# Three of seven reads of the first down products by ScalarE and Pool; the norms' last two squares summed by TensorE

## The chip, the cores and the metric

The kernel runs on one core of a Trainium2 chip, in one launch. The metric is the device time of that core in microseconds (us): 1850.29 us, the median of three executions (1849.76 to 1850.89). One more execution was taken by the profiler and took 1851.48 us; all rows below come from it.

## The reference

One decoder layer over 1024 tokens of width 1024, in fp32, with one sequence:

```
h = modulate(rms_norm(x, norm_ffn1), mod[0], mod[1])
x = x + 0.5 * mod[2] * swiglu(h, gate1, up1, down1)
h = modulate(rms_norm(x, norm_mix), mod[3], mod[4])
x = x + mod[5] * (concat(gated_delta_rule(h), pooled(h)) @ w_out)
h = modulate(rms_norm(x, norm_ffn2), mod[6], mod[7])
x = x + 0.5 * mod[8] * swiglu(h, gate2, up2, down2)
out = rms_norm(x, final_norm)
swiglu(h) = (silu(h @ w_gate) * (h @ w_up)) @ w_down      # hidden width 2816
rms_norm(x, g) = x * rsqrt(mean(x * x) + 1e-6) * g
```

## The kernel before, in words

Activations lie transposed: sixteen tiles A[d, h] of 128 features by 512 tokens, d from 0 to 7 and h the half of the tokens. Every fp32 product is three matmuls on operands that are split into a high and a low fp32r part (tiles named `split` for weights; pairs in H, G, U and zs for what moves). "Stage 1" and "stage 2" are the two SwiGLU blocks; between them stands the mixer.

**Seven products.** The big products of a stage take 2x2 blocks and spend seven block products where eight are usual. `seven` (l. 872) goes through them in the order p1, p2, p5, p6, p3, p7, q4. p1, p6, p7 and q4 of one step share one PSUM bank (tile `mm`) and add onto it, p5 and p3 share another (`po`), and p2 has one of its own (`po`). So p6 may begin only when p1's sum was read, p7 when p6's was, and p3 when p5's was; these are the flags ("read", stage, step, product). Steps 0 to 19 of a stage are the gate and up products, steps from 20 on (`NP1`) are the down products. Step 20 sums over one pair of hidden blocks, 21 over two, 22 over three, then four, so a product of these steps is 3, 6, 9 and 12 matmuls of 512 columns.

**Reading a down product.** `down_read` (l. 979) adds each of the seven sums, times the gate `fg`, onto the tile of A that it belongs to, by one `scalar_tensor_tensor` of VectorE: p1 and p2 onto block (0,0), p6 and p3 onto (0,1), p5 and p7 onto (1,1), q4 onto (1,0). The tiles of A were put away in DRAM and come back by `rest_load` (l. 1186, tiles `A<-xpark` and `A<-rest`), each into a slot that a task of the stage before it has given back.

**The two norms between the stages.** `square_task` (l. 1296) squares the eight feature tiles of one half of the tokens on ScalarE; GpSimd (Pool) adds each onto the first one. `norm_task` (l. 1309) then waits for the last of these additions, lets TensorE take the column sums against a column of ones (four columns of 128 tokens, by `column_sums`, l. 310), VectorE makes mean and epsilon of them (`rx`), Pool raises to the power -1/2, VectorE spreads the result on a diagonal (`row_diag`), and TensorE multiplies it by ones into R, the scale of every token on all partitions (`aux<-cv,ones`). From R and A come the next products' H. This runs for the mixer's norm (1) and the second SwiGLU's norm (2), each for both halves; the final norm has code of its own. TensorE meanwhile has the last products of the stage in its queue.

**The order.** The code is written as generator tasks that yield what they need and what they cost: `("V", 0.77)` asks for 0.77 us of VectorE, S is ScalarE, G Pool, D a DMA on SyncE's queue; `need` takes a buffer, `flag` waits for an event. A class `Order` (l. 36) plays these tasks against each other on the build machine, and the instructions are issued in the order that comes out. This fixes the order on every engine. All calls pass one helper, so that each row of the profile names line L161; what a row belongs to is told by its tiles.

Of the kernel before, what the change touches and what calls it, by code (L numbers as in the profile page):

```python
# [11 lines left out]
ALU = mybir.AluOpType  # L12
AX = mybir.AxisListType

P = 128
D = 1024
T = 1024
HT = 512
KT = D // P
# [3 lines left out]
EPS = 1e-6  # L23
# [12 lines left out]
class Order:  # L36
# [18 lines left out]
    def spawn(self, gen, rank):  # L55
        self.seq += 1
        self.tasks.append({"gen": gen, "rank": rank, "seq": self.seq, "ready": self.t, "ask": None, "last": None, "end": self.t})
        return self.tasks[-1]

    def put(self, what, n=1):  # L60
        self.events.append((self.t, "put", what, n))
# [81 lines left out]
def hybrid_layer_kernel(  # L143
# [22 lines left out]
    V, S, G, PE = Pin(nc.vector, "V"), Pin(nc.scalar, "S"), Pin(nc.gpsimd, "G"), Pin(nc.tensor, "PE")  # L166
    uid = [0]

    def nm(s):
        uid[0] += 1  # L170
        return f"{s}_{uid[0]}"
# [12 lines left out]
    def bank(tag="mm"):  # L184
        bufs = {"mm": 2, "aux": 3, "rec": 1, "po": 2}[tag]
        return psum.tile([P, HT], F32, tag=tag, bufs=bufs, name=nm(tag))

    def pm():
        return work.tile([P, HT], F32, tag="pm", bufs=4, name=nm("pm"))

    def cvt(n=HT):
        return work.tile([P, n], F32, tag="cv", bufs=4, padded_shape=[P, 528], name=nm("cv"))
# [11 lines left out]
    def cst(shape, name):  # L204
        return const.tile(shape, F32, tag=name, name=name)
# [12 lines left out]
    for i, s in enumerate(LEVELS):  # L218
        nb = P // (2 * s)
        v = lmask[:, i].rearrange("p (b two s) -> p b two s", two=2, s=s)[:, :, 0, :]  # L220
# [22 lines left out]
    A = {}  # L243
# [10 lines left out]
    ps = bank("po")  # L254
# [9 lines left out]
    fg = [cst([P, 8], f"fg{i}") for i in range(2)]  # L264
# [30 lines left out]
    def ad():  # L295
        return work.tile([P, HT], F32, tag="ad", bufs=6, name=nm("ad"))
# [7 lines left out]
    def xtile(k, h, src):  # L304

        if k >= KT // 2:
            return gtile(8 + 2 * (k - KT // 2) + h)
        return ztile() if h else ad()

    def column_sums(parts, ps):  # L310
        for n in range(parts[0].shape[1] // P):
            for e, t in enumerate(parts):
                PE.matmul(ps[:, n : n + 1], lhsT=t[:, n * P : (n + 1) * P], rhs=ones[:, 0:1], start=(e == 0), stop=(e == len(parts) - 1))
# [10 lines left out]
    def row_diag(r):  # L324
        diag = cvt()
        V.tensor_tensor(diag.rearrange("p (n j) -> p n j", n=4), ident.unsqueeze(1).broadcast_to([P, 4, P]), r.unsqueeze(2).broadcast_to([P, 4, P]), op=ALU.mult)
        return diag
# [43 lines left out]
    spawn, put, mark = order.spawn, order.put, order.set  # L371

    def need(what, n=1):
        return ("need", what, n)

    def flag(*key):
        return ("flag", key)
# [28 lines left out]
    def release(i):  # L406
        free.append(i)
        put("tmp")
# [358 lines left out]
    rest = (xpark, {})  # L767
# [16 lines left out]
    NP1 = 2 * (NPAIR - 1)  # L784
# [194 lines left out]
    def down_read(st, n, v, ps, banks):  # L979
        d = 2 * plans[st][n]["d"]  # L980
        todo = {"p1": (0, 0), "p2": (0, 0), "p5": (1, 1), "p6": (0, 1), "p3": (0, 1), "p7": (1, 1), "q4": (1, 0)}[v]
        a = d + todo[0], todo[1]
        yield flag("mod", 8 if st else 2)
        yield flag("rest", st, a)
        yield ("V", 0.77)
        V.scalar_tensor_tensor(A[a], ps, fg[st][:, a[0] : a[0] + 1], A[a], op0=ALU.mult, op1=ALU.add)
        if v in ("p2", "p3"):
            put("po")
        elif v == "q4":
            put("mm")  # L990
        else:
            mark(("read", st, n, v))
        if n == len(plans[st]) - 1 or d // 2 not in [e["d"] for e in plans[st][n + 1 :]]:
            mark(("summed", st, a, v))
# [220 lines left out]
    def last_pair():  # L1215
        for h in range(2):
            for d in range(KT):
                yield need("mm")
                ps = bank()
                yield flag("unit", "last", d // 2)  # L1220
                u = unit["last", d // 2]
                for f in range(2):
                    yield flag("G", 0, NS, f, h)
                    for e, (a, b) in enumerate(((0, 0), (0, 1), (1, 0))):
                        yield ("PE", 0.2267)
                        PE.matmul(ps, lhsT=u[:, a, f, (d % 2) * P : (d % 2 + 1) * P], rhs=ring[0, NS, f, h][b], start=f == e == 0, stop=f == 1 and e == 2)
                if h == 1 and d % 2:
                    put("split")
                spawn(last_read(ps, d, h), 0.8)
            spawn(norm_task(h, 1, last_parts[h], A, 1), 1.5)  # L1230

    def last_read(ps, d, h):
        for v in {(0, 0): ("p2",), (0, 1): ("p3",), (1, 0): ("q4",), (1, 1): ("p7",)}[d % 2, h]:
            yield flag("summed", 0, (d, h), v)
        yield ("V", 0.66)
        V.scalar_tensor_tensor(A[d, h], ps, fg[0][:, d : d + 1], A[d, h], op0=ALU.mult, op1=ALU.add)
        put("mm")
        spawn(square_task(1, h, d, last_parts[h], A[d, h]), 2)
        yield ("D", 0.5)
        park[d, h] = dram.tile([P, HT], F32, tag=f"park{d}_{h}", name=nm("park"))  # L1240
        nc.sync.dma_start(out=park[d, h], in_=A[d, h])
# [42 lines left out]
    def low_task(k, h, i, xn):  # L1284
        yield ("S", 0.61)
        ht = htile(k, h)
        H[k, h] = ht
        b = mod[3 * i][:, k : k + 1]
        S.activation(ht[:, 0], xn, AF.Identity, bias=b)
        yield ("V", 0.66)  # L1290
        V.scalar_tensor_tensor(ht[:, 1], xn, b, ht[:, 0].bitcast(F32), op0=ALU.add, op1=ALU.subtract)
        if i == 1:
            put("pm")
        mark(("H", i, k, h))

    def square_task(st, h, i, parts, src):
        yield need("cv" if i else "U")
        yield ("S", 0.52)
        sq = cvt() if i else work.tile([P, HT], F32, tag="U", bufs=4, name=nm("acc"))
        S.activation(sq, src, AF.Square)  # L1300
        parts.append(sq)
        if i:
            yield flag("sum", st, h, i - 1)
            yield ("G", 1.6)
            G.tensor_tensor(parts[0], parts[0], sq, op=ALU.add)
            put("cv")
        mark(("sum", st, h, i))

    def norm_task(h, i, parts, src, rank):
        yield flag("sum", i, h, KT - 1)  # L1310
        yield flag("acol", i)
        yield need("aux", 2)
        yield need("cv")
        yield ("PE", 0.9)
        ps = bank("aux")
        column_sums(parts[:1], ps)
        yield ("V", 0.07)
        r = small.tile([P, 4], F32, tag="rx", bufs=2, name=nm("rx"))
        V.tensor_scalar(r, ps[:, 0:4], 1.0 / D, EPS, op0=ALU.mult, op1=ALU.add)
        put("aux")  # L1320
        put("U")
        yield ("G", 1.0)
        G.tensor_tensor(r, r, neghalf[:, 0:4], op=ALU.pow)
        yield ("V", 0.6)
        diag = row_diag(r)
        yield ("PE", 0.86)
        R = bank("aux")
        PE.matmul(R, lhsT=ones, rhs=diag, start=True, stop=True)
        put("cv")
        for k in range(KT):  # L1330
            if i == 1:
                yield need("pm")
            elif k < KT // 2:
                yield need("zs" if h else "ad")
            elif h == 0:
                yield flag("mix", 3, 1)
            yield ("V", 0.66)
            xn = pm() if i == 1 else xtile(k, h, src)
            XN[k, h] = xn
            V.scalar_tensor_tensor(xn, src[k, h], acol[i][:, k : k + 1], R, op0=ALU.mult, op1=ALU.mult)  # L1340
            if i == 2:
                release(OUT_TILES[h][k])
            spawn(low_task(k, h, i, xn), rank)
        put("aux")
# [446 lines left out]
    def out_task(ps, d, h):  # L1791
        yield flag("mod", 5)
        yield ("V", 0.66)
        V.scalar_tensor_tensor(A[d, h], ps, mod[5][:, d : d + 1], A[d, h], op0=ALU.mult, op1=ALU.add)
        put("mm")
        spawn(square_task(2, h, d, out_parts[h], A[d, h]), 2)
        yield ("D", 0.5)
        rest[1][d, h] = dram.tile([P, HT], F32, tag=f"rest{d}_{h}", name=nm("rest"))
        nc.sync.dma_start(out=rest[1][d, h], in_=A[d, h])
# [206 lines left out]
    for j, piece in enumerate(((0, 0, HT), (1, 0, 256), (1, 256, HT))):  # L2006
        h, lo, hi = piece
        parts, ds = [], list(range(KT))[:: -1 if j % 2 else 1]
        for d in ds:
            if d // 2 not in kept:  # L2010
                kept[d // 2] = wunit2(last_src(ffn2_down, d // 2))
            ps = bank()[:, : hi - lo]
# [3 lines left out]
            a = A[d, h][:, lo:hi]  # L2016
# [32 lines left out]
```

## Time and profile before

| | us | share |
|---|---|---|
| median of three executions | 1850.29 | |
| profiled execution | 1851.48 | |
| its span | 1849.8 | |
| TensorE (PE) busy | 1796.6 | 97% |
| VectorE (DVE) busy | 1400.4 | 76% |
| ScalarE (ACT) busy | 768.4 | 42% |
| GpSimd (POOL) busy | 286.0 | 15% |

Busy time is that of an engine's instructions; what is left of the span is the time in which the engine waited. In a row of the timeline the first two columns are start and duration in us, then engine, line, operation, output and inputs by tile names, shape and count; a bracket at the end gives the idle time ahead of the row and what ended it. PEclk is the granted share of TensorE's full clock. Stage 1's down products run from 483 us on, norm 1 stands at 690 to 735, the mixer's inner part at 735 to 1125, norm 2 at 1125 to 1210, stage 2's down products begin at 1600.

### The profile page before, as it was taken

To read this page: it belongs to the slowest core of one execution; us is meant where nothing else is said; L and a number is where in the kernel's file an instruction comes from. 1 tells how busy PE (TensorE), PEld (TensorE's weight loads), DVE (VectorE), ACT (ScalarE), POOL (GpSimd) and SP (SyncE) were. 2 spreads that over 40 slices of the span, in tenths; PEclk is the share of its full clock that TensorE was granted. 3 is DMA by queue.
4 is the path that set the end of the run, shared out by engine and by line. 5 is a ranking of instruction groups with operands and counts; after the bars stand their busy time and mean duration, and the time that the engine had idled before them with its cause. 6 is when DMAs were issued, how large, how long until landed. Compare 5 with 4: busy or idle time off the path is not lost.

```text
span 1849.8 us, 25078 instructions
## 1 busy us (share of the span) xinstructions
PE 1796.6 (97%) x8511; PEld 1481.7 (80%) x8511; DVE 1400.4 (76%) x2440; ACT 768.4 (42%) x1519; POOL 286.0 (15%) x228
## 2 busy tenths in 40 slices
PE   7999999999999999999999999999999999999997
PEld 6788878888788877788888878878878888778876
DVE  4997888887778878988787666677787666776666
ACT  5454444443422224662443354444445444422225
POOL 2231121201100003120211122212111111100004
PEclk9999999999999999999999999999999999999999
DMA  9534676574679933331111155334455543667722
GB/s 315 182 120 159 207 225 206 182 229 132 201 242 331 310 96 104 103 78 43 31 48 49 41 173 159 95 123 139 154 180 181 174 137 126 206 207 253 238 70 92
DMA packets 307551, 293.29 MB, mean 159 GB/s; under 512 B 28053, under 2 KB 215506, under 8 KB 307424
## 3 DMA queue, kind: packets, MB, share of 16 engines
q1 hardware_dynamic: 306848, 290.57, 49.5%
q8 instruction: 67, 1.10, 0.2%
q0 software_dynamic: 576, 1.13, 0.2%
q14 instruction: 60, 0.49, 0.1%
HBM read 208.53 MB, written 83.10 MB: 158 GB/s over the span
## 4 chain that ended last, share of the span: by engine, by line
PE 83%; DVE 11%; issue 2%; ACT 1%; POOL 1%; DMA 1%; ACTq 0%; POOLq 0%; DVEq 0%
PE mm L161 47%; PE po L161 27%; PE aux L161 7%; PE rec L161 3%; DVE pm L161 2%; DVE A L161 2%; DVE ad L161 2%; DVE split L161 2%; DVE G L161 1%; DVE cv L161 1%; DVE H L161 1%; ACT A L161 0%; DMA G<-in_gdn_norm 0%; DVE zs L161 0%; ACT junk L161 0%
## 5 line engine op out<-in xcount | busy, mean ns | idle before, releaser
L161 PE MATMUL mm<-H,split 128*128 128x512 f32 (+1 forms) x3096 | 766.2, 395 | 9.6 <-DVE H L161 4.0
L161 PEld LDWEIGHTS mm<-H,split 128*128 128x128 f32 x3096 | 568.4, 189 | 127.1 <-DVE H L161 5.1
L161 PE MATMUL po<-H,split 128*128 128x512 f32 x1584 | 388.1, 392 | 4.4 <-DVE H L161 3.0
L161 PEld LDWEIGHTS po<-H,split 128*128 128x128 f32 x1584 | 297.3, 189 | 69.2 <-DVE H L161 4.2
L161 PE MATMUL mm<-G,split 128*128 128x512 f32 x1440 | 342.5, 390 | 4.3 <-ACT split L161 4.3
L161 PEld LDWEIGHTS mm<-G,split 128*128 128x128 f32 x1440 | 269.9, 188 | 61.2 <-ACT split L161 5.2
L161 ACT CAST split<-pm 128x512 fp32r<-128x512 f32 (+3 forms) x264 | 151.7, 582 | 329.0 <-DVE pm L161 322.8
L161 POOL TENSOR_TENSOR A<-A,A 128x512 f32<-128x512 f32 x80 | 130.7, 1644 | 692.2 <-DVE A L161 593.5
L161 DVE TENSOR_TENSOR split<-pm,split 128x512 fp32r<-128x512 f32 (+3 forms) x264 | 176.6, 676 | 45.1 <-ACT split L161 44.5
L161 ACT CAST split<-raw 128x512 fp32r<-128x512 f32 (+2 forms) x199 | 117.6, 596 | 194.0 <-PE mm L161 104.0
L161 PE MATMUL po<-U,split 128*128 128x512 f32 x480 | 155.5, 390 | 2.1 <-DVE A L161 2.1
L161 DVE SCALAR_TENSOR_TENSOR A<-mm,fg,A 128x512 f32<-128x512 f32 (+1 forms) x144 | 103.0, 719 | 65.8 <-PE mm L161 64.5
L161 DVE TENSOR_TENSOR split<-raw,split 128x512 fp32r<-128x512 f32 (+2 forms) x199 | 132.3, 675 | 21.1 <-ACT split L161 20.7
L161 DVE TENSOR_TENSOR A<-A,A 128x512 fp32r<-128x512 f32 (+1 forms) x180 | 124.1, 697 | 4.3 <-ACT A L161 1.2
L161 PEld LDWEIGHTS po<-U,split 128*128 128x128 f32 x480 | 90.1, 188 | 22.0 <-issue 1.7
L161 POOL TENSOR_TENSOR acc<-acc,cv 128x512 f32<-128x512 f32 (+1 forms) x46 | 56.1, 1219 | 292.2 <-ACT cv L161 291.2
L161 ACT CAST split<-cv 128x512 fp32r<-128x512 f32 (+1 forms) x96 | 57.1, 595 | 94.0 <-PE po L161 52.2
L161 DVE TENSOR_TENSOR A<-A,po 128x512 f32<-128x512 f32 x86 | 58.8, 684 | 46.4 <-PE po L161 43.2
L161 PE MATMUL po<-zs,split 128*128 128x512 f32 x240 | 93.4, 389 | 0.0
L161 DVE SCALAR_TENSOR_TENSOR ad<-ad,cs,ad 128x512 f32<-128x512 f32 x98 | 82.8, 845 | 3.5 <-DMA ad<-in_w_ada 2.6
L161 DVE TENSOR_TENSOR split<-cv,split 128x512 fp32r<-128x512 f32 (+1 forms) x96 | 62.7, 653 | 27.7 <-ACT split L161 27.7
L161 ACT CAST A<-A 128x512 fp32r<-128x512 f32 x120 | 72.8, 619 | 25.9 <-DVE A L161 25.2
(279 smaller groups left out, 1881.2 us busy)
## 6 DMA issues: line engine op xcount, KB each, us to landing
gd<-A SPq DMA_DIRECT2D x240, 256.0 KB, 3.9
H<-gd SPq DMA_DIRECT2D x144, 256.0 KB, 3.9
ad<-in_w_ada SPq DMA_DIRECT2D x112, 256.0 KB, 3.3
raw<-in_ffn_gate SPq DMA_DIRECT2D x88, 256.0 KB, 4.0
cv<-in_ffn_up SPq DMA_DIRECT2D x80, 256.0 KB, 4.4
G<-gd SPq DMA_DIRECT2D x64, 256.0 KB, 3.7
raw<-in_w_in SPq DMA_DIRECT2D x40, 256.0 KB, 3.2
cv<-in_ffn_down SPq DMA_DIRECT2D x32, 256.0 KB, 4.0
```

The lines of the kernel that those rows point to most:

```text
L161: ins = f(*args, **kwargs)
```

## The change

Two edits. In `down_read`, p1, p6 and p7 of steps 20, 21 and 22 (nine of the reads of each stage) are no longer one VectorE instruction: ScalarE multiplies the PSUM sum by the gate into a tile of the ring `ad`, sets the read flag, and Pool adds that tile onto A. In `square_task` and `norm_task`, the squares of the last two feature tiles are no longer added by Pool; TensorE takes the column sums of three tiles (the sum so far and the two squares) into twelve columns, and VectorE adds the three by one `tensor_reduce` ahead of the `tensor_scalar` that was there. The planner's price of a Pool addition in `square_task` goes from 1.6 to 1.3.

```
@@ down_read
         a = d + todo[0], todo[1]
         yield flag("mod", 8 if st else 2)
+        if n < NP1 + 3 and v in ("p1", "p6", "p7"):
+            yield need("ad")
+            yield ("S", 0.62)
+            t = ad()
+            S.mul(t, ps, fg[st][:, a[0] : a[0] + 1])
+            mark(("read", st, n, v))
+            yield flag("rest", st, a)
+            yield ("G", 1.4)
+            G.tensor_tensor(A[a], A[a], t, op=ALU.add)
+            put("ad")
+            return
         yield flag("rest", st, a)
         yield ("V", 0.77)
         V.scalar_tensor_tensor(A[a], ps, fg[st][:, a[0] : a[0] + 1], A[a], op0=ALU.mult, op1=ALU.add)
@@ square_task
         parts.append(sq)
-        if i:
+        if 0 < i < KT - 2:
             yield flag("sum", st, h, i - 1)
-            yield ("G", 1.6)
+            yield ("G", 1.3)
             G.tensor_tensor(parts[0], parts[0], sq, op=ALU.add)
             put("cv")
         mark(("sum", st, h, i))
@@ norm_task
     def norm_task(h, i, parts, src, rank):
-        yield flag("sum", i, h, KT - 1)
         yield flag("acol", i)
         yield need("aux", 2)
+        ps = bank("aux")
+        for j, e in enumerate((KT - 3, KT - 2, KT - 1)):
+            yield flag("sum", i, h, e)
+            yield ("PE", 0.9)
+            column_sums((parts[e if j else 0],), ps[:, 4 * j : 4 * j + 4])
+            if j:
+                put("cv")
         yield need("cv")
-        yield ("PE", 0.9)
-        ps = bank("aux")
-        column_sums(parts[:1], ps)
-        yield ("V", 0.07)
+        yield ("V", 0.3)
         r = small.tile([P, 4], F32, tag="rx", bufs=2, name=nm("rx"))
-        V.tensor_scalar(r, ps[:, 0:4], 1.0 / D, EPS, op0=ALU.mult, op1=ALU.add)
+        V.tensor_reduce(r, ps[:, 0:12].rearrange("p (j n) -> p n j", n=4), axis=AX.X, op=ALU.add)
+        V.tensor_scalar(r, r, 1.0 / D, EPS, op0=ALU.mult, op1=ALU.add)
         put("aux")
```

Because the planner plays all tasks again, instructions move on every engine, most of all inside the mixer. Three places follow, two on VectorE and one on TensorE. A tile's number at the end of its name tells one tile from the next; numbers differ between the two kernels.

VectorE in stage 1's down step 22, before: `zs_4612` is the low part of p5's last operand, `po_4744` is p2's sum and `po_4765` is p5's.

```order
619 L161 TENSOR_TENSOR H_0_942_4605<-A_911_4495,H_0_942_4605 128x512
620 L161 TENSOR_TENSOR zs_4612<-A_919_4529,U_4611 128x512
621 L161 SCALAR_TENSOR_TENSOR A_937_4588<-mm_4700,fg_165,A_937_4588 128x512
622 L161 SCALAR_TENSOR_TENSOR A_906_4476<-mm_4582,fg_165,A_906_4476 128x512
623 L161 TENSOR_TENSOR pm_4755<-raw_4499,raw_4570 128x384
624 L161 TENSOR_TENSOR split_4748<-cv_4652,split_4748 128x512
625 L161 SCALAR_TENSOR_TENSOR A_937_4588<-po_4744,fg_165,A_937_4588 128x512
626 L161 TENSOR_TENSOR split_4761<-pm_4755,split_4761 128x384
627 L161 TENSOR_TENSOR split_4770<-raw_4580,split_4770 128x384
628 L161 TENSOR_TENSOR G_949_4627<-A_924_4547,G_948_4626 128x512
629 L161 SCALAR_TENSOR_TENSOR A_979_4743<-po_4765,fg_165,A_979_4743 128x512
630 L161 TENSOR_TENSOR split_4785<-cv_4698,split_4785 128x512
```

The same place after: `zs_4694` is the low part, `po_4738` p2's sum and `po_4765` p5's.

```order
616 L161 SCALAR_TENSOR_TENSOR A_960_4679<-po_4738,fg_165,A_960_4679 128x512
617 L161 TENSOR_TENSOR split_4757<-pm_4740,split_4757 128x384
618 L161 TENSOR_TENSOR split_4762<-cv_4622,split_4762 128x512
619 L161 TENSOR_TENSOR split_4770<-raw_4582,split_4770 128x384
620 L161 TENSOR_TENSOR zs_4694<-A_919_4529,U_4693 128x512
621 L161 TENSOR_TENSOR G_973_4719<-A_931_4575,G_972_4718 128x512
622 L161 TENSOR_TENSOR H_1_980_4742<-A_880_4332,H_1_980_4742 128x512
623 L161 TENSOR_TENSOR G_990_4778<-A_890_4378,G_989_4777 128x512
624 L161 TENSOR_TENSOR H_1_992_4784<-A_955_4656,H_1_992_4784 128x512
625 L161 TENSOR_TENSOR split_4804<-cv_4753,split_4804 128x512
626 L161 TENSOR_TENSOR pm_4824<-cv_4653,cv_4670 128x512
627 L161 SCALAR_TENSOR_TENSOR A_995_4794<-po_4765,fg_165,A_995_4794 128x512
```

The low part stood five rows ahead of the read of p2's sum and now stands four rows behind it; the read of p5's sum came nine rows after the low part and now comes seven rows after it, with six additions from SBUF to SBUF in between.

TensorE at norm 1, first half of the tokens, after: `acc` is the sum of six squares, the two `cv` are the last squares, `aux<-cv,ones` is R, and `mm<-H_1` are stage 1's last products.

```order
1857 L161 MATMUL mm_6453<-H_1_1247_6092,split_6299 128x512
1858 L161 MATMUL aux_6444<-ones,acc_6356 128x1 x4
1859 L161 MATMUL aux_6444<-ones,cv_6442 128x1 x4
1860 L161 MATMUL aux_6444<-ones,cv_6455 128x1 x4
1861 L161 MATMUL mm_6453<-H_1_1247_6092,split_6299 128x512 x2
1862 L161 MATMUL mm_6453<-H_1_1252_6124,split_6299 128x512 x3
1863 L161 MATMUL mm_6483<-H_1_1247_6092,split_6303 128x512 x3
1864 L161 MATMUL mm_6483<-H_1_1252_6124,split_6303 128x512 x3
1865 L161 MATMUL mm_6497<-H_1_1247_6092,split_6303 128x512 x3
1866 L161 MATMUL aux_6504<-cv_6492,ones 128x512
```

Before, twelve such matmuls stood between the column sums and R, and nine behind R; now fourteen stand between them, and the column sums come earlier among the products.

VectorE at the start of stage 2, before: `split_11125` is the first weight split of the product that follows norm 2 (step 0's p1), `zs` and `G` are operands of stage 2's other products.

```order
1676 L161 TENSOR_TENSOR zs_11132<-ad_10606,U_11131 128x512
1677 L161 SCALAR_TENSOR_TENSOR G_2323_11028<-G_2323_11028,mod_159,ad_10593 128x512
1678 L161 TENSOR_TENSOR G_2347_11147<-G_2317_11003,G_2346_11146 128x512
1679 L161 SCALAR_TENSOR_TENSOR G_2325_11035<-G_2325_11035,mod_159,ad_10606 128x512
1680 L161 TENSOR_TENSOR G_2349_11159<-G_2323_11028,G_2348_11158 128x512
1681 L161 SCALAR_TENSOR_TENSOR G_2246_10639<-G_2246_10639,mod_159,G_2315_10996 128x512
1682 L161 TENSOR_TENSOR A_2351_11168<-A_2351_11168,aux_11025 128x512
1683 L161 SCALAR_TENSOR_TENSOR G_2249_10653<-G_2249_10653,mod_159,G_2317_11003 128x512
1684 L161 TENSOR_TENSOR G_2354_11175<-G_2325_11035,G_2353_11174 128x512
1685 L161 SCALAR_TENSOR_TENSOR G_2253_10667<-G_2253_10667,mod_159,G_2323_11028 128x512
1686 L161 TENSOR_TENSOR split_11125<-raw_10873,split_11125 128x512
```

The same place after: `split_11170` is that first split.

```order
1668 L161 TENSOR_TENSOR zs_11151<-ad_10613,U_11150 128x512
1669 L161 TENSOR_TENSOR G_2349_11144<-G_2324_11026,G_2348_11143 128x512
1670 L161 TENSOR_TENSOR split_11164<-raw_10954,split_11164 128x512
1671 L161 TENSOR_TENSOR G_2353_11158<-G_2326_11033,G_2352_11157 128x512
1672 L161 SCALAR_TENSOR_TENSOR G_2329_11055<-G_2329_11055,mod_159,ad_10600 128x512
1673 L161 TENSOR_TENSOR split_11170<-raw_10912,split_11170 128x512
```

From the last `zs` the split stood ten rows on and now stands five; counted from the first of that work (`db`, l. 1030) it stood 22 rows on and now stands 16.

## Rows read from the trace of the kernel before

**Rows 1.** Windows: length, busy us (instructions) of PE, PEld, DVE, ACT, POOL; PEclk, DMA

```profile
480.00:526.00 46.00, 40.94 (x177) 32.40 (x176) 42.78 (x76) 16.77 (x35) 3.85 (x3) 1.00 0.58 175
...
775.00:1100.00 325.00, 320.73 (x1869) 271.50 (x1868) 250.79 (x614) 143.32 (x400) 55.80 (x48) 1.00 0.24 65
```

**Rows 2.** Timeline of PE, stage 1's down steps 20 to 22

```profile
487.98 0.93 PE L161 MATMUL po<-H,split 128*128 128x512 f32 x3 [0.42 <-DVE A L161]
491.08 0.96 PE L161 MATMUL mm<-G,split 128*128 128x512 f32 x3 [2.17 <-ACT split L161]
...
504.63 2.12 PE L161 MATMUL mm<-H,split 128*128 128x512 f32 x8 [2.01 <-DVE H L161]
...
510.68 2.20 PE L161 MATMUL mm<-G,split 128*128 128x512 f32 x9
512.72 1.75 PE L161 MATMUL po<-H,split 128*128 128x512 f32 x7
514.93 0.74 PE L161 MATMUL po<-H,split 128*128 128x512 f32 x2 [0.46 <-DVE H L161]
```

**Rows 3.** Groups by shape: the read by DVE, one by ACT, Pool's addition

```profile
L161 POOL TENSOR_TENSOR A<-A,A 128x512 f32<-128x512 f32 x80 | 130.7, 1644 | 692.2 <-DVE A L161 593.5 <-issue 53.4 <-DMA gd<-A 26.8
L161 DVE SCALAR_TENSOR_TENSOR A<-mm,fg,A 128x512 f32<-128x512 f32 x128 | 95.6, 749 | 64.5 <-PE mm L161 63.3
...
L161 ACT ACTIVATE A<-mm 128x512 f32<-128x512 f32 x23 | 13.8, 598 | 39.0 <-PE mm L161 37.9 <-issue 1.1
```

**Rows 4.** Timeline of DVE and POOL at 481 and 489 us

```profile
481.25 0.28 DVE L161 TENSOR_TENSOR pm<-pm,raw 128x128 f32<-128x128 f32 x1
...
489.01 0.74 DVE L161 SCALAR_TENSOR_TENSOR A<-po,fg,A 128x512 f32<-128x512 f32 x1
489.67 0.97 DVE L161 TENSOR_TENSOR pm<-raw,raw 128x128 f32<-128x128 f32 x1
...
489.24 1.26 POOL L161 TENSOR_TENSOR A<-A,A 128x512 f32<-128x512 f32 x1 [5.09 <-DVE H L161]
```

**Rows 5.** Timeline of DVE and POOL at 1219 us

```profile
1219.64 0.69 DVE L161 TENSOR_TENSOR split<-pm,split 128x512 fp32r<-128x512 f32 x1
1220.24 1.78 DVE L161 TENSOR_TENSOR pm<-cv,cv 128x512 f32<-128x512 f32 x1
...
1219.86 5.00 POOL L161 TENSOR_TENSOR A<-A,A 128x512 f32<-128x512 f32 x3 [15.06 <-DVE A L161]
```

**Rows 6.** Timeline of PE, stage 2's down step 21, product p1

```profile
1609.63 3.81 PE L161 MATMUL mm<-H,split 128*128 128x512 f32 x9
```

**Rows 7.** Timeline of PE at norm 1: column sums, R, the mixer's first products

```profile
703.42 0.95 PE L161 MATMUL aux<-ones,acc 128*128 128x1 f32 x8
704.23 3.02 PE L161 MATMUL mm<-H,split 128*128 128x512 f32 x12
708.47 1.10 PE L161 MATMUL aux<-cv,ones 128*128 128x512 f32 x2 [1.21 <-DVE cv L161]
709.00 2.62 PE L161 MATMUL mm<-H,split 128*128 128x512 f32 x9
711.47 0.50 PE L161 MATMUL po<-H,split 128*128 128x512 f32 x1
714.05 1.45 PE L161 MATMUL po<-H,split 128*128 128x512 f32 x5 [2.08 <-DVE H L161]
...
718.98 0.85 PE L161 MATMUL mm<-H,split 128*128 128x512 f32 x3
```

**Rows 8.** Timeline of DVE and POOL at norm 1, between column sums and R

```profile
706.55 1.77 DVE L161 TENSOR_TENSOR cv<-ident,rx 128x512 f32<-128x512 f32 x1 [0.57 <-POOL rx L161]
...
705.48 1.04 POOL L161 TENSOR_TENSOR rx<-rx,neghalf 128x4 f32<-128x4 f32 x1
```

**Rows 9.** Timeline of PE at norm 2's end

```profile
1206.67 17.77 PE L161 MATMUL mm<-H,split 128*128 128x512 f32 x70 [3.31 <-DVE split L161]
1224.27 4.02 PE L161 MATMUL po<-H,split 128*128 128x512 f32 x17
```

## The prediction

> **What bounds the kernel now.** I began with the page's first two parts: TensorE is busy for 1796.6 of 1849.8 us, so only 53 us of the span are TensorE waiting, and any gain has to come out of those, or out of stretches in which it works at a lower granted clock. The windows then tell where the waits are. In the stretch in which stage 1's down products begin, TensorE works 40.94 of 46 us while VectorE works 42.78 [rows 1]: this is one of the few places where VectorE is the fuller engine. The timeline of TensorE names each wait there: 0.42, 2.17, 2.01 and 0.46 us, together 5.06, each ended by VectorE or by a split made from VectorE's result [rows 2]. In the mixer, 775 to 1100 us, TensorE works 320.73 of 325 us [rows 1]. The two norms between have waits of their own: 1.21 and 2.08 us at norm 1 [rows 7] and 3.31 us at norm 2 [rows 9].
>
> **The down products.** Per stage nine reads leave VectorE. One is 0.749 us [rows 3], so VectorE gets 6.7 us back in each stage. For each one ScalarE gets an instruction from PSUM to SBUF (0.598 us for such a one) and Pool an addition from SBUF to SBUF, 1.644 us in the mean of its 80 [rows 3] and 1.26 us where nothing is in its way [rows 4]. ScalarE is busy for 16.77 of 46 us and Pool for 3.85 [rows 1], so 5.4 and 11.3 us find room on these engines. The question is what Pool's additions do to VectorE. While the one at 489.24 runs, the read of a PSUM sum at 489.01 takes its usual 0.74 us, but the subtraction at 489.67, with both inputs in SBUF, takes 0.97 us where its like takes 0.28 at 481.25 [rows 4]. While three additions run from 1219.86 on, a VectorE instruction of that kind takes 1.78 us, against 0.69 just before [rows 5]. So an addition of Pool holds one SBUF instruction of VectorE for 0.69 to 1.09 us. Nine of them cost VectorE 6.2 to 9.8 us for the 6.7 that it saves: a balance of -0.5 to +3.1 us per stage, on the engine that is fuller there.
>
> The Trainium skill says the same of the two engines in "SBUF — State Buffer", section "SBUF: two separate sides": Pool and a VectorE instruction with two SBUF inputs want one shared port pair, whoever starts first keeps it for the whole instruction, and the other waits. "Perfetto Trace Analysis", section "Optimizing Scalar/DVE Operations", adds that offloading between the two might not help. The two rows above agree with that; by this rule the term comes out at the value below, and if it did not apply it would be the lower end.
>
> Where this meets TensorE is read from the new order of VectorE and from these durations, product by product. (1) In steps 20 and 21 one read of 0.74 us no longer stands ahead of the splits that end the waits of 0.42 and 2.17 us: -0.8. (2) Step 21's read of p2's sum works on the tile that Pool must first add p1's sum to: ScalarE and Pool need 0.60 + 1.26 us for what VectorE did in 0.75, and behind it in VectorE's queue stands the read of p5's sum, without which p3 may not start: +1.1. (3) The wait of 2.01 us inside step 22's p1 is for a low half of H behind a long row of VectorE work, from which two reads are gone and into which one hold has come, 2 x 0.75 - 0.7 to 1.1: -0.7. (4) The low half `zs` of p5's operand in step 22 stood ahead of the read of p2's sum and now stands behind it and three splits. From p2's end VectorE needs 0.75 for the read, 0.55 + 0.69 + 0.55 for the splits (a 384 wide one estimated at four fifths of the 0.69 of [rows 5]) and 0.69 for `zs`, 3.2 us. TensorE has seven matmuls of p5 to do meanwhile; nine take 2.04 us from start to start (510.68 to 512.72 in [rows 2]), one 0.227, seven 1.6. That is a new wait of 1.6, and with half a hold, since four of the five have two SBUF inputs, 2.1. (5) The read of p5's sum now has six SBUF instructions between it and `zs`, which start 0.60 apart [rows 5]: 3.6 + 0.75 us, while TensorE has two matmuls of p5 and nine of p6, 2.5 us. That is a wait of 1.8 ahead of p3, where there was one of 0.46 [rows 2]: +1.3. Sum: -0.8 + 1.1 - 0.7 + 2.1 + 1.3 = +3.0 us per stage.
>
> The ends: if the holds fall where nothing waits, (1) to (3) can at best remove all 5.06 us and only the waits that the order itself forces, 1.6 and 1.8, stay: -1.6. If every hold costs 1.09 us and lies in front of something that TensorE waits for, VectorE's +3.1 and the wait of 1.8 add: +4.9. Stage 2 has the same order and the same waits, and behind the 2.17 us wait nine matmuls take 3.81 us there [rows 6] where nine take 2.20 in stage 1 [rows 2]: 1.6 us of lower clock that are already paid. I take +3.0 for both stages, 6.0 together.
>
> **The norms.** Column sums of four columns take TensorE 0.81 us (703.42 to 704.23, [rows 7]); twelve take 2.43, so each of the four halves adds 1.62 us of TensorE work, 6.5 in all, and nothing hides it, since TensorE is the bound there. `tensor_reduce` over twelve columns is not in the trace; the row nearest to it, a `tensor_scalar` on four columns, is a matter of tenths, and it stands on a chain that has slack below, so I give it 0.2 and see it as hidden.
>
> At norm 1, first half, two of Pool's additions leave the chain between the last square and the column sums. The sums come earlier among stage 1's last products, and 14 matmuls (3.2 us) instead of 12 stand between them and R. The chain from sums to R took 4.2 us before (704.23 to 708.47, [rows 7]), of which Pool's power was 1.04, begun late behind an addition of squares, and the diagonal was held for 1.77 [rows 8] instead of 0.69. Without those additions it is about 0.2 + 0.3 + 1.04 + 0.2 + 0.69, 2.4 us, and fits into the 3.2. So the wait ahead of R goes, and since R comes earlier against the products behind it, the wait of 2.08 ahead of the mixer's first products goes too, with the slow matmuls behind it. From start to start: 704.23 to 714.05 is 9.82 us with 22 matmuls of 0.227 (5.0) and R's 0.53, so 4.3 lost; 714.05 to 718.98 is 4.93 us for 14 matmuls (3.2), so 1.8 lost to the clock [rows 7]. 6.1 come back, 2 x 1.62 are paid: -2.8. Bounds: all lost time stays, +3.2; or it goes and one half's sums find a gap, -4.5.
>
> At norm 2 the first half adds 1.62 and the second 1.62, TensorE being full up to 1203 us. The wait of 3.31 at 1206.67 is for a split on VectorE [rows 9] that was put behind much of the work for stage 2's other operands; in the new order it stands six instructions earlier against that work, some 4 us by the 0.60 to 0.75 us of one, and TensorE comes 3.2 us later. So the wait goes, and with it the 17.77 us that 70 matmuls took behind it [rows 9], against 70 x 0.227 + 0.17 = 16.0: -1.7. Sum 3.24 - 3.31 - 1.7 = -1.8; bounds -3 and +3.2 (nothing removed).
>
> **The mixer** is planned anew in whole. It has 4.3 us of TensorE waits in 325 us [rows 1], which is the most that a better order can give; I take 0, with 4.3 to both sides.
>
> **Sum.** 6.0 - 2.8 - 1.8 + 0 = +1.4 us on the profiled execution's 1851.48 us, 1852.9. That execution is 1.2 us above the median, so in the median's terms it is 1850.3 + 1.4 = 1851.7 us.
>
> **Rivals.**
> - *The holds find gaps (faster).* Pool has time and its additions needn't be soon; both down starts come to their lower end, -1.6, and with shorter waits stage 2's 1.6 us of lower clock go too. -3.2 - 1.6 - 2.8 - 1.8 = -9.4: 1840.9. For it speaks that most of a down stretch is splits and combinations with slack; against it that VectorE has only 3.2 us free in 46 [rows 1].
> - *The holds decide (slower).* Every addition of Pool holds an SBUF instruction for the whole 1.09 us at the head of VectorE's queue in the down starts: 2 x 4.9, less the norms' 4.6, and stage 1 falls to the lower clock as stage 2 does, +1.6. +6.8: 1857.1. It decides from about +4.2 per down start on. For it speaks [rows 5], where three in a row were held so; against it [rows 4], where one cost 0.69.
> - *The column sums buy nothing (slower).* At norm 2 the split keeps its distance to the norm's chain, which itself ends later; nothing is removed there, +3.2: 6.0 - 2.8 + 3.2 = +6.4, 1856.7.
> - *The mixer drifts*, by its 4.3 us to one side: 1847.4 or 1856.0.
>
> **How the numbers follow.** A difference under 0.2% (3.7 us) can't be told from none. Forecast 0.40, the holds find gaps 0.27, the holds decide 0.17, column sums 0.06, mixer 0.10, half to each side (its better half counted as faster, since it would come with part of the first rival). Faster 0.27 + 0.05 = 0.32, same 0.40, slower 0.17 + 0.06 + 0.05 = 0.28. The forecast's own range is 1848 to 1855; to hold 8 in 10 it reaches to 1842 and 1858, most of the way to the rivals on both sides.
>
> **What would show it.** In TensorE's timeline at the down starts: new waits ahead of step 22's p5 (on `zs`, about 2 us) and p3 (on A, about 1.8), and the 2.01 us wait shorter. In VectorE's: instructions with SBUF inputs at 1 to 1.8 us under Pool's additions, PSUM reads still at 0.75. At the norms: column sums of 2.4 us, no wait at R, none ahead of the mixer's first `po`, full clock behind it, and no wait at the start of stage 2's first product. The forecast is wrong if the down stretches are shorter than before, if the waits at the norms stay, or if the mixer's windows change by more than 4 us.

## The result, and the profile after

The changed kernel takes 1859.44 us (median of five, 1858.15 to 1862.24), the kernel before in the same comparison 1849.85 us: 9.6 us slower, ratio 1.0054 with a 95% interval of 1.0042 to 1.0065. Forecast were 1851.7 us, within 1842 to 1858. The sign of "slower" had a chance of 0.28; the time lies 1.4 us above the range.

The profiled execution took 1859.67 us with a span of 1858.0. The start of the same matmul in both traces tells in which stretch the 8.2 us of the spans came:

| stretch, by the matmul that begins it | before | after | difference | forecast |
|---|---|---|---|---|
| from 0 to the first down product | 485.36 | 482.38 | -3.0 | 0 |
| down start 1, to 517.59 | 32.23 | 35.62 | +3.4 | +3.0 |
| norm 1, 685.48 to the mixer's `rec<-H` at 733.76 | 48.28 | 53.27 | +5.0 | -2.8 |
| mixer and norm 2, to 1224.27 | 490.51 | 491.42 | +0.9 | -1.8 |
| down start 2, 1603.12 to 1636.80 | 33.68 | 35.41 | +1.7 | +3.0 |

Up to 485 us both kernels give TensorE the same instructions in the same order; the 3.0 us there differ from execution to execution (by 0.1 to 2.9 in the eleven profiles below) and belong to no edit. Part of them is TensorE's clock: it stands at its lower level from 49.9 to 56.7 us before and only to 53.3 after, which is 1.7 us of work at most. Without the 3.0 us the profile agrees with the medians to about 1.6 us. The down starts cost about what was forecast. The norms, forecast as a gain of 4.6 us, cost 5.9.

TensorE's timeline of the kernel after at norm 1 (start, duration, engine, line, operation, count) answers to [rows 7]:

```profile
699.12 0.94 PE L161 MATMUL aux<-ones,acc 128*128 128x1 f32 x8
699.93 1.93 PE L161 MATMUL aux<-ones,cv 128*128 128x1 f32 x16
701.72 5.05 PE L161 MATMUL mm<-H,split 128*128 128x512 f32 x14
706.61 1.02 PE L161 MATMUL aux<-cv,ones 128*128 128x512 f32 x2
707.06 5.79 PE L161 MATMUL mm<-H,split 128*128 128x512 f32 x21
713.46 1.66 PE L161 MATMUL mm<-H,split 128*128 128x512 f32 x6 [0.61 <-DVE A L161]
714.96 1.32 PE L161 MATMUL po<-H,split 128*128 128x512 f32 x5
716.11 0.95 PE L161 MATMUL aux<-ones,acc 128*128 128x1 f32 x8
717.56 1.05 PE L161 MATMUL aux<-ones,cv 128*128 128x1 f32 x8 [0.51 <-ACT cv L161]
718.88 1.87 PE L161 MATMUL aux<-ones,cv 128*128 128x1 f32 x8 [0.27 <-ACT cv L161]
720.61 0.77 PE L161 MATMUL po<-H,split 128*128 128x512 f32 x1
```

Both waits that were to go are gone: R (`aux<-cv,ones`) has no idle time ahead of it, and none of 2.08 us stands ahead of the mixer's first `po`. But the fourteen matmuls behind the first column sums take 4.89 us from start to start, 0.349 us each, where 0.227 is the full pace. The windows behind all four column sums (window, length, then busy us of PE, PEld, DVE, ACT, POOL, and PEclk, the granted share of full clock) say why:

```profile
701.72:706.61 4.89, 4.89 (x17) 3.85 (x17) 2.78 (x6) 1.25 (x2) 1.92 (x2) 0.65 0.14 52
720.61:726.02 5.41, 5.41 (x14) 4.28 (x15) 5.38 (x12) 2.17 (x3) 1.02 (x1) 0.53 0.38 96
1130.98:1135.63 4.65, 4.65 (x15) 3.66 (x15) 1.03 (x3) 0.00 (x0) 1.02 (x1) 0.63 0.36 105
1179.72:1184.12 4.40, 4.40 (x14) 3.52 (x14) 1.03 (x3) 0.00 (x0) 1.02 (x1) 0.62 0.94 268
```

Behind each of the four, TensorE works without a pause and at 0.53 to 0.65 of its clock, mostly at the lower of its two levels (1.2 of 2.4 GHz). With 14, 13, 13 and 12 product matmuls in them at 0.227, the four windows lose 1.7, 2.5, 1.7 and 1.7 us: 7.6 us. What TensorE did just before was in each case 24 matmuls of one column each, from 699.12 to 701.72 for the first; the second 24 have the waits shown above among them, the two bursts of norm 2 one product matmul each.

At the first down start the same view shows the forecast waits; it answers to [rows 2]:

```profile
484.74 0.96 PE L161 MATMUL po<-H,split 128*128 128x512 f32 x3 [0.17 <-DVE A L161]
486.40 0.73 PE L161 MATMUL mm<-G,split 128*128 128x512 f32 x2 [0.69 <-ACT split L161]
487.89 0.50 PE L161 MATMUL mm<-G,split 128*128 128x512 f32 x1 [0.76 <-DVE split L161]
...
495.63 1.61 PE L161 MATMUL po<-H,split 128*128 128x512 f32 x6 [0.52 <-DVE A L161]
498.44 3.82 PE L161 MATMUL mm<-H,split 128*128 128x512 f32 x15
...
509.22 0.50 PE L161 MATMUL po<-zs,split 128*128 128x512 f32 x1 [3.34 <-DVE zs L161]
509.56 0.39 PE L161 MATMUL po<-U,split 128*128 128x512 f32 x1
509.79 3.30 PE L161 MATMUL mm<-G,split 128*128 128x512 f32 x9
513.59 2.53 PE L161 MATMUL po<-H,split 128*128 128x512 f32 x9 [0.50 <-DVE A L161]
```

The wait on `zs` is there, 3.34 us long, and the nine matmuls of p6 behind it take 3.30 us where nine took 2.20 [rows 2]. VectorE and Pool in the same stretch answer to [rows 4]:

```profile
483.26 1.43 DVE L161 SCALAR_TENSOR_TENSOR A<-po,fg,A 128x512 f32<-128x512 f32 x2
...
489.20 0.43 DVE L161 TENSOR_TENSOR pm<-pm,cv 128x256 f32<-128x256 f32 x1
489.67 1.40 DVE L161 TENSOR_TENSOR pm<-cv,pm 128x256 f32<-128x256 f32 x1
490.99 1.52 DVE L161 TENSOR_TENSOR split<-pm,split 128x256 fp32r<-128x256 f32 x1
...
483.33 1.30 POOL L161 TENSOR_TENSOR A<-A,A 128x512 f32<-128x512 f32 x1 [2.15 <-DMA H<-gd]
...
489.20 3.02 POOL L161 TENSOR_TENSOR A<-A,ad 128x512 f32<-128x512 f32 x2 [2.05 <-ACT ad L161]
```

Two of the new additions run from 489.20 on. The two VectorE instructions under them take 1.40 and 1.52 us where their like take 0.41 to 0.43. Two reads of PSUM sums, from 483.26 on, keep their 0.72 each while another of Pool's additions runs.

### The profile page after: what moved, and what is told of

The parts are those of the page before. It is cut to its first block, busy times and chain, and to the rows that moved or that the text cites. A ratio compares the mean times of both kernels' runs of the same rounds, so it can differ in the third digit from the quotient of the medians.

```text
span 1858.0 us, 25229 instructions
## 1 busy us (share of the span) xinstructions
PE 1808.7 (97%) x8575; PEld 1490.3 (80%) x8575; DVE 1404.8 (76%) x2426; ACT 781.9 (42%) x1539; POOL 301.6 (16%) x238
## 4 chain that ended last, share of the span: by engine, by line
PE 83%; DVE 11%; issue 3%; ACT 2%; POOL 1%; DMA 1%; ACTq 0%; POOLq 0%; DVEq 0%
PE mm L161 46%; PE po L161 26%; PE aux L161 7%; DVE pm L161 3%; PE rec L161 3%; DVE A L161 2%; DVE split L161 2%; DVE ad L161 2%; DVE cv L161 1%; DVE G L161 1%; DVE H L161 1%; ACT A L161 0%; ACT junk L161 0%; DVE zs L161 0%; DMA G<-in_gdn_norm 0%
## 5 line engine op out<-in xcount | busy, mean ns | idle before, releaser
L161 DVE TENSOR_TENSOR split<-pm,split 128x512 fp32r<-128x512 f32 (+3 forms) x264 | 183.5, 703 | 48.5 <-ACT split L161 47.9
L161 DVE SCALAR_TENSOR_TENSOR A<-mm,fg,A 128x512 f32<-128x512 f32 (+1 forms) x126 | 89.7, 715 | 63.4 <-PE mm L161 62.3
L161 POOL TENSOR_TENSOR acc<-acc,cv 128x512 f32<-128x512 f32 (+1 forms) x38 | 45.7, 1202 | 251.9 <-ACT cv L161 251.0
```

What stands on the lines that cost most here:

```text
L161: ins = f(*args, **kwargs)
```

## The experiments

All differences below are against the kernel before in the same comparison. The table gives, from each profile, the same stretches as above (us against the profile of before).

| kernel | median | before | ratio, 95% interval | start | down 1 | norm 1 | mixer, norm 2 | down 2 |
|---|---|---|---|---|---|---|---|---|
| changed kernel | 1859.44 | 1849.85 | 1.0042 to 1.0065 | -3.0 | +3.4 | +5.0 | +0.9 | +1.7 |
| e1 sums tripled | 1864.24 | 1850.09 | 1.0053 to 1.0084 | -0.2 | +4.2 | +4.1 | +5.2 | 0.0 |
| e2 norm alone | 1855.67 | 1850.09 | 1.0016 to 1.0037 | -1.2 | 0.0 | +5.1 | +0.9 | -1.4 |
| e3 reads alone | 1852.87 | 1850.09 | 1.0008 to 1.0028 | -2.9 | +3.2 | -1.6 | -1.2 | +1.7 |
| e4 sums apart | 1857.05 | 1850.09 | 1.0023 to 1.0049 | -2.6 | +3.9 | -0.3 | +3.5 | +1.7 |
| e5 tiny adds | 1845.54 | 1849.49 | 0.9971 to 0.9990 | -2.6 | -2.2 | -1.6 | +0.1 | -3.6 |
| e6 zs early | 1852.99 | 1849.49 | 1.0008 to 1.0026 | -1.1 | +2.0 | -1.6 | +1.6 | +0.6 |
| e8 split early | 1842.69 | 1849.49 | 0.9959 to 0.9978 | -0.4 | -0.1 | +0.2 | -5.2 | +2.8 |
| e9 one square | 1843.70 | 1849.49 | 0.9958 to 0.9978 | -2.3 | +1.2 | -2.7 | -2.2 | +1.7 |
| e10 norm apart, split | 1849.01 | 1850.45 | 0.9974 to 0.9996 | -0.1 | 0.0 | -0.1 | -1.8 | +2.8 |
| e11 all apart, split | 1853.69 | 1850.45 | 1.0003 to 1.0022 | -1.2 | +3.4 | -0.2 | -1.7 | +1.7 |
| e12 splits first | 1838.36 | 1850.45 | 0.9908 to 0.9941 | -2.5 | -0.6 | -1.6 | -5.2 | -2.4 |

One warning for reading it: where the instructions of a stretch are those of before (down 1 in e1, e2, e8; down 2 in e1, e2, e8, e10; norm 1 in e8), the profiles still differ by -1.4 to +4.2 us. In each such case a stretch of low clock behind a wait of about 2 us is there in one execution and not in another. A single profile tells of a down start no more than that; the medians carry the verdicts. The profiled execution isn't the median one either: it took 1850.40 us in e3, 1841.60 in e5, 1848.93 in e8 and 1851.91 in e10, so the stretches need not add up to the medians' difference.

**e1, the column sums alone.** The sums of before are taken three times:

```
         column_sums(parts[:1], ps)
+        column_sums(parts[:1], ps[:, 4:8])
+        column_sums(parts[:1], ps[:, 8:12])
```

> The kernel before with one thing more: each of the four column sums of the two middle norms is taken three times (twelve columns, of which the last eight are not used); Pool's additions, the reads and the planner's prices are as before, so no instruction moves. Theory A (the sums slow the clock): behind each of the four sums TensorE runs at the lower of its two levels for some 8 to 11 matmuls, 1.5 to 2.1 us each, beside the 4 x 1.62 us of the sums themselves; at norm 1 the waits behind stay as they are. Slower by 10 to 13 us. Theory B (the slow stretches in the changed kernel came from the waits around its sums, on squares and on VectorE): the sums cost only their own time, slower by 5 to 7 us, and no low-clock stretch starts behind a column sum.

Measured +14.2 us, for 8 x 0.81 = 6.5 us of added work; that is above the range of either theory. At norm 2's first half a sum with no wait in it is followed by

```profile
1135.48 2.73 PE L161 MATMUL aux<-ones,acc 128*128 128x1 f32 x24
1138.07 4.83 PE L161 MATMUL mm<-H,split 128*128 128x512 f32 x13
```

4.67 us for 13 matmuls, 1.7 too many, as at the same place of the changed kernel. Behind norm 1's second sum the clock falls too, and 1.7 us are lost from 727.83 to 732.72. Behind norm 1's first sum it doesn't:

```profile
707.21 2.73 PE L161 MATMUL aux<-ones,acc 128*128 128x1 f32 x24
709.81 3.03 PE L161 MATMUL mm<-H,split 128*128 128x512 f32 x12
...
718.81 2.50 PE L161 MATMUL po<-H,split 128*128 128x512 f32 x5 [2.09 <-DVE H L161]
```

The slow matmuls from 718.81 on stand behind the wait of 2.09 us, as they did in the kernel before [rows 7]. Behind norm 2's second sum there was no fall either. So theory A holds at two sums of four: the burst alone can bring the clock down, and doesn't every time. The sums and these two falls are 9.9 us; another 4.2 stand in the first down start, whose instructions are those of before.

**e2 and e3, the two edits apart.** e2 is the changed kernel with `down_read` as before, e3 the kernel before with the eleven new lines of `down_read`.

> The norms' edit alone, reads as before. Theory A: the norms carry +6 to +7 of the changed kernel's 8 to 10 us (norm 1 +5, norm 2 +1.5), with four low-clock stretches behind the column sums; slower than before by 5 to 8 us. Theory B (the norms' edit itself is about free or a gain, as forecast at -4.6, and the loss comes from the reads' edit through the order): between -5 and +2 us.

> The reads' edit alone, norms as before. Theory A: the down starts cost +3.4 and +1.7 us as in the changed kernel (a wait of about 3.3 on zs in step 22, holds of VectorE under Pool's additions), the norms and the mixer nothing but replanning: slower than before by 4 to 6 us. Theory B (the reads' edit carries the loss): 8 to 10 us.

Measured +5.6 and +2.8; the two sum to 8.4 of 9.6. The norms carry two thirds of that sum, with +5.1 and +0.9 much as in the changed kernel, and slow stretches behind all four sums again. The reads' own cost came out smaller than either theory had it, though its down starts lose 3.2 and 1.7 in the profile.

**e4, the sums apart.** In the changed kernel's `norm_task`:

```
             yield flag("sum", i, h, e)
+            if j:
+                yield ("wait", 2.0)
             yield ("PE", 0.9)
```

> The changed kernel with a planned pause of 2.0 us before the second and third column sum of each norm, so that some nine product matmuls stand between them; the work is the same. Theory A: where no stretch of narrow matmuls is long, the clock stays at its upper level; the four slow stretches of 1.5 to 2.1 us go: 5 to 8 us faster than the changed kernel, about +2 to +4 against before. Theory B (waits): no faster than the changed kernel within 2 us.

Measured +7.0 against before, so 2.6 gained where 5 to 8 were expected. The clock did what theory A says: the windows of norm 1 and of norm 2 (columns as above) stand at full clock, with the same 24 narrow matmuls per sum in three pieces of 0.81 us and six to ten product matmuls between them,

```profile
700.00:735.00 35.00, 33.66 (x167) 27.28 (x167) 29.66 (x47) 17.53 (x31) 9.55 (x7) 1.00 0.30 99
1124.00:1190.00 66.00, 66.00 (x312) 54.59 (x311) 39.46 (x60) 24.96 (x41) 11.65 (x9) 1.00 0.44 136
```

and norm 1 came from +5.0 to -0.3. What was given back stands at stage 2's first product, where the new plan put the splits late again:

```profile
1211.19 17.74 PE L161 MATMUL mm<-H,split 128*128 128x512 f32 x70 [3.31 <-DVE split L161]
```

That is the wait of [rows 9] to the hundredth, with its slow matmuls. So the sums' clock and the splits' place are two things, and the next runs took the second by itself.

**e8, the early splits.** In the kernel before, one rank:

```
-            spawn(unit_split(key), 3)
+            spawn(unit_split(key), 1 if key in (len(units) - 2, len(units) - 1) else 3)
```

> The kernel before, with the planner's rank of the last two weight splits ahead of stage 2 lowered (3 to 1), so that they stand 14 places earlier on VectorE; nothing else. If the wait of 3.31 us at 1206.67 and the slow clock behind it hung on these splits alone (as the changed kernel's missing wait suggests), 4 to 5.2 us faster than before. If the wait is only moved to another operand: within 2 us of before.

Measured -6.8 us: faster than both kernels, by an edit that has nothing to do with the change. The wait and its slow matmuls were worth 5.2 at most; where the rest comes from wasn't settled. The product starts with no wait and at full clock:

```profile
1202.45 16.48 PE L161 MATMUL mm<-H,split 128*128 128x512 f32 x72
```

**e5, the hold.** e3 with Pool's nine additions per stage on 4 of 512 columns:

```
-            G.tensor_tensor(A[a], A[a], t, op=ALU.add)
+            G.tensor_tensor(A[a][:, 0:4], A[a][:, 0:4], t[:, 0:4], op=ALU.add)
```

> The reads' edit alone, with Pool's nine additions per stage on the first 4 of 512 columns only (the rest of the three sums is left out); planner and order are those of the reads' edit alone, and every wait on Pool stays. Theory H (the long additions hold VectorE): without them the holds go, the down starts fall from +3.2 and +1.7 us against before to about 0 to -1.6 each; the wait on zs shrinks from 3.3 to about 1.6 us. Theory O (the order alone): the waits on zs and on A stay as long as they are, and each down start stays within 1 us of +3.2 and +1.7.

Measured -3.9 against before, 6.7 us less than e3's +2.8; in the profiles the down starts fall from +3.2 and +1.7 to -2.2 and -3.6, about 5.4 each. By the medians the two starts together are 6.7, so one is worth 3.4 to 5.4 us. The order is that of e3. In e3's first start (above the dots) and e5's (below):

```profile
489.28 1.57 DVE L161 TENSOR_TENSOR pm<-pm,cv 128x256 f32<-128x256 f32 x1
498.38 0.75 DVE L161 SCALAR_TENSOR_TENSOR A<-po,fg,A 128x512 f32<-128x512 f32 x1 [1.19 <-POOL A L161]
...
487.61 0.42 DVE L161 TENSOR_TENSOR pm<-pm,cv 128x256 f32<-128x256 f32 x1
494.44 0.75 DVE L161 SCALAR_TENSOR_TENSOR A<-po,fg,A 128x512 f32<-128x512 f32 x1 [0.42 <-POOL A L161]
```

Ahead of `zs` six rows with SBUF inputs take 0.95 to 1.15 us less in e5 than in e3, 6.5 in all. The short additions also end sooner, and VectorE's read waits 0.42 us for one instead of 1.19; e5 doesn't separate this from the holds, but it is 0.8 us at most. The wait on `zs` is now what its order alone forces:

```profile
504.20 0.50 PE L161 MATMUL po<-zs,split 128*128 128x512 f32 x1 [1.46 <-DVE zs L161]
```

1.46 us, against a worked out 1.6. Theory H, in the main.

**e6, `zs` early.** In `direct_task`'s spawn, rank 1.0 in place of 2.8 for p5 of the last pair.

> The reads' edit alone, with the planner's rank of p5's last operand lowered (2.8 to 1.0), which puts zs fourteen places earlier on VectorE, ahead of the read of p2's sum. Theory O: the 3.3 us wait on zs goes and with it the low clock behind it (1.3 to 1.5 us); the down starts fall by 2 to 4 us each, to +1 and -1 against before. Theory H: VectorE has the same work and the same holds, so the wait moves to the next operand; the down starts change by less than 1.5 us.

Measured +3.5, e3 having +2.8: nothing gained. In the profile the wait on `zs` is gone and waits on H have come, in the same step:

```profile
503.70 2.12 PE L161 MATMUL mm<-H,split 128*128 128x512 f32 x8 [1.64 <-DVE H L161]
509.29 0.73 PE L161 MATMUL po<-H,split 128*128 128x512 f32 x2 [1.87 <-DVE H L161]
```

VectorE has the same work and the same holds, and the wait moves: theory H again.

**e9, the smallest form of the norms' edit.** e8, and in norm 1's first half alone only the last square goes to TensorE, eight columns in one piece (the loop of the change with `KT - 2` and `KT - 1`, under `i == 1 and h == 0`, with the change's planner price of 1.3).

> The kernel before with the early splits of the run above and the norms' edit in a small form: only norm 1's first half, only its last square goes to TensorE (eight columns instead of four or twelve). Theory A (the length of the burst of narrow matmuls counts): a burst of 1.6 us leaves the clock up or nearly so; norm 1 gains 3 to 5 us (the waits of 1.2 and 2.1 us and the slow matmuls behind them go, 0.8 is paid), norm 2 gains 4 to 5: 7 to 10 us faster than before. If eight columns slow the clock too, norm 1 gains 1 to 3: 5 to 8 us faster.

Measured -5.8, short of theory A's 7 to 10. Behind these sixteen narrow matmuls (1.7 us) the clock stayed up, and the waits of 1.2 and 2.1 us at norm 1 are gone. Norm 1 gained 2.7 us in the profile, mixer and norm 2 gave 3.0 of e8's 5.2 back; the whole is no better than e8. Why the new plan of the mixer costs that was not looked into.

**e10 and e11, the parts put together.** The pauses of e4 and the split rank of e8, in e2 and in the changed kernel.

> The norms' edit alone, with the sums apart (pauses of 2.0 us) and the early splits. If the norms' loss is the clock behind the bursts and the waits inside them, and the wait at stage 2's first product is the splits' alone, the parts add up: norm 1 about -0.3, norm 2 +3.2 for the sums and -5.2 for the splits: 1 to 4 us faster than before, and 7 to 10 faster than the norms' edit alone. If something else in the norms' edit costs, it stays at +2 or above.

> The changed kernel with both repairs, sums apart and early splits. If the loss has the parts found so far, what is left is the reads' edit, +3.2 and +1.7 in the down starts, with -2 from the norms: +1 to +4 us against before, 5 to 8 faster than the changed kernel.

Measured -1.4 and +3.2, both as the parts add up. e10 is 7.0 us better than e2, e11 6.4 better than the changed kernel. In none of the four does stage 2's first product wait, so these 7.0 and 6.4 us are the cleanest price of the bursts: the low clock and the waits inside the sums. The granted clock is 1.00 through both norms of e10 and e11, as in e4: no fall behind twelve sums in pieces, against eight falls behind eight bursts in the changed kernel and e2. What is left of e11's loss is the reads' edit (e11 less e10: 4.7; e3 alone: 2.8).

**e12, the way the trace points for the down starts.** e8, and

```
-            spawn(split_weights(st, n, v), 1 if n < 2 else 1.7 if NP1 <= n < NP1 + 4 else 3)
+            spawn(split_weights(st, n, v), 1 if n < 2 else 0.7 if NP1 <= n < NP1 + 3 else 3)
```

> The kernel before with the early splits ahead of stage 2, and the planner's rank of the weight splits of down steps 20 to 22 lowered from 1.7 to 0.7, so that they go ahead of the reads on VectorE; the reads' edit isn't in it. If the waits of 2.17 us (a split) and 2.01 us (H) in the down starts can be taken away by order alone, 3 to 5 us faster per down start than before, 10 to 15 in all with the early splits; if VectorE is the bound there, the waits move to the reads: within 1.5 us per down start, 5 to 8 us faster than before in all.

Measured -12.1 us (four executions), the fastest of all: 1838.36, 5.3 us further against its own kernel before than e8. The waits of 2.17 and 2.01 us are gone, others have come for them,

```profile
487.36 0.93 PE L161 MATMUL po<-H,split 128*128 128x512 f32 x3 [2.27 <-DVE A L161]
...
498.05 1.63 PE L161 MATMUL po<-H,split 128*128 128x512 f32 x6 [1.11 <-DVE A L161]
```

so part of the wait moved to the reads. The profile shows -0.6 and -2.4 in the down starts; that is less than the medians' 5.3, and where the rest comes from wasn't settled.

## Why the prediction was wrong

**The step that failed** is the price of the column sums: "twelve take 2.43, so each of the four halves adds 1.62 us of TensorE work", with "full clock behind it" among what was to be seen. The work was sized right (2.60 us for the first, waits apart). What was left out is that TensorE comes out of the burst at its lower clock: 7.6 us over four sums, in place of the 1.8 and 1.7 us of slow matmuls that the forecast took away. e1 shows it with the burst alone at two sums of four; e4, e10 and e11, with the same sums in pieces, don't have it at any.

**Norm 1, -2.8 forecast, +5.0 measured.** The 6.1 us of waits and slow matmuls went as forecast. In their place came, from start to start: 1.8 for the first sum (2.60 less 0.81); 3.7 for the second (716.11 to 720.61 less 0.80), of which 1.6 is work, 1.2 waits for its last squares on ScalarE, 0.51 and 0.27 among them, and 0.9 the lower clock, which sets in before the last eight narrow matmuls (1.73 us from start to start); 1.7 and 2.5 of low clock; and 1.6 between 707.06 and 713.46, where 21 matmuls have 4.8 us of work. That last one is a wait for VectorE's read of A at 712.67. Ahead of it in VectorE's queue an instruction on H took 1.78 us from 710.97 on, about 1.0 more than its like, while Pool added squares of the second half. Before, such an instruction (1.45 us at 712.55) stood behind the last of these reads. This account is read from the traces; no run tested it. 11.3 less 6.1 is 5.2, close to the 5.0. Sums in the planned order stand where their squares are ready by the planner's clock; a sum split in three can wait three times.

**Norm 2 and the mixer, -1.8 forecast, +0.9 measured.** The wait and its slow matmuls went (-5.2) as forecast, and the sums cost +3.6, near the 3.2 forecast; low clock behind both sums, 1.7 each, was not forecast. That leaves -0.9 for the mixer, forecast as 0. The gain of 5.2 us was not the edit's own: e8 has it from a rank, and e4 lost it with the norms' edit still in.

**The down starts, +3.0 each forecast, +3.4 and +1.7 measured.** The mechanism was right, and e5 shows its size: the holds are worth 3.4 (medians) to 5.4 us (profiles) per start, where the forecast had 4.6 between its value (+3.0) and its lower end (-1.6; measured without them, -2.2 and -3.6). The second of these includes the 1.6 us of low clock of [rows 6], which e5's profile doesn't have. By the Trainium skill, "SBUF — State Buffer", section "SBUF: two separate sides", of a VectorE instruction with two SBUF inputs and one of Pool the one that starts second waits for the whole of the other; e5's profile agrees, since with additions of four columns the VectorE instructions of that stretch are back at their usual length. Within the term the sizes shifted: the early waits lost 1.0 (0.8 forecast), p3's wait in step 21 came at 0.5 (1.1), H's 2.01 went wholly (0.7), and the one on `zs` is 3.3 (2.1). p3's in step 22 is 0.5 behind a p6 that the low clock made 1.1 us longer, so p3 starts 1.6 late, near the 1.8 forecast; in e3's first start p6 runs at full clock and the wait is 1.58. The low clock there cost next to nothing, since p3 would have waited. That +3.4 came so near to +3.0 is in part luck: the terms for H and `zs` were 1.3 and 1.2 off, to opposite sides. Stage 2 lost less because the kernel before already paid 1.6 us of low clock there [rows 6].

**The rivals.** "The column sums buy nothing" came nearest in place, at the norms, but for another reason: it had the split keep its distance. "The holds find gaps" did not happen; e5 is what it would have been. "The holds decide" had the size of one hold nearly right (1.09; 0.95 to 1.15 in e3), and not the +4.9 per start.

## What to carry to other kernels

Work on TensorE isn't priced by its time alone: a run of many one-column matmuls can cost as much again in the clock behind it (here 1.7 us and more behind 1.6 us of added work), so keep such runs short or set product matmuls between them. An addition handed to Pool isn't free while VectorE has SBUF work to do; price it by the VectorE instruction that it holds. And before crediting an edit with a wait that disappears, ask whether it is the edit or the order it came with: here one rank took the same wait away for nothing.

## What the runs showed of the hardware

The lower clock came without TensorE being idle. The Trainium skill, "TensorE: Matmul & The Clock Gate", section "HAM oscillation — how this bites in real kernels", puts the falls down to gaps between matmuls; here the window 699.12 to 701.72 is full of instructions and the fall follows it. In pieces of 0.81 us with six to ten product matmuls between (e4, e10, e11), or as sixteen in one piece (e9), the same kind of matmul left the clock up. In one piece of 24, e1 had falls behind two of four.

Behind waits of about 2 us the fall is a matter of the execution: the 3.81 us of [rows 6] have no counterpart in e2's trace, whose down start 2 has the same instructions and is 1.4 us shorter, and e1's down start 1, with the instructions of before, is 4.2 us longer by two such stretches.
